# Weight splitting of the second layer done ahead of it: parts made during the first layer's MLP, kept in DRAM, loaded as parts

## The chip, the cores and the metric

The kernel runs on one core of one Trainium2 chip. The metric is the device time of one execution in microseconds (us). TensorE (PE) multiplies matrices; VectorE (DVE) and ScalarE (ACT) do elementwise work and empty the matmul results; GpSimd (POOL) computes a few reciprocal roots; SyncE (SP) issues almost all DMAs. Each engine takes its instructions in one fixed order and waits at the first one that isn't ready.

## The reference

Two layers of a decoder trunk over 1024 tokens of width 1024, all in float32. For each layer:

```
h = rms_norm(x, g_pre_mix);  z = h @ w_in            # one projection for three head groups
mix = concat(mLSTM(z), sliding_window_GQA(z), differential_attention(z)) @ w_out
x = x + rms_norm(mix, g_post_mix)
h2 = rms_norm(x, g_pre_mlp); u = square(relu(h2 @ w_up))
x = x + rms_norm(u @ w_down, g_post_mlp)
```

w_in has 2824 columns, w_up and w_down have 4096 hidden units.

## The kernel before

Every large matmul is computed from a high and a low part of both operands, so that the product keeps nearly float32 accuracy: `hi` is the value cast to the matmul's type (float32r), `lo` is the remainder, and the three products hi·hi, hi·lo and lo·hi are summed in PSUM. A weight tile is therefore a pair. It is made by `load_w` (line 103): for each half of 512 columns a DMA on SP brings the plain weights into a `raw` buffer (line 109, tensor `rw`), ACT casts them to `hi` (line 93) and DVE subtracts to get `lo` (line 94). There are two `raw` buffers of 512 columns, so one tile of 1024 columns can be waiting in plain form while its final buffers are still in use; the load then needs no final buffer, only the cast and the subtraction do. For w_up the cast also multiplies by a gain (lines 116 and 117).

Each layer runs in this order. First come the projections: `proj_tiles` (matmul line 286, tensors `wt`, results `pt`) for 13 tiles of w_in, in groups of one to four; `p_g2` (matmuls `pg`, weights `wg`, line 358) for the gates and values; `nat_group` (matmuls `pn`, weights `wv`) for two groups more. Differential attention (`diff1` to `diff4`) has the higher priority and is spread between the projections. Then sliding-window attention (`swa1`, `swa2`) and the mLSTM (`mlstm1` to `mlstm3`) run side by side, with the first half of the output projection (`out_group`, matmul line 849, weights `wo`, `woh`, `wol`); its second half follows with the post-norm (`post_mix`). Then the MLP runs in eight chunks of four hidden tiles: an up phase of 192 matmuls (line 1013, results `pu`, emptied on ACT at line 1016 as `r`) and a down phase of 192 (line 1058, results `pd`, added to `acm` on DVE at line 1069, or copied on ACT at line 1067 in the first chunk).

The final buffers of weights come from small pools: `whl` has two pairs, `wd` and `ws` four single tiles each. Most groups of projections use both `whl` pairs, so the next group's first tile can only be written when the running group has finished with a pair. The `mm` pool gives `pu`, `pt`, `pg` and `pn` two PSUM buffers; the down phase has four.

The order of each engine is set by a scheduler that walks the program with priorities (`ahead(n)` raises them) and fills free places of an engine with whatever is ready and has lower priority, however much later it stands in the source.

Of the kernel before, what the change touches and what calls it, by code (L numbers as in the profile page):

```python
# [10 lines left out]
F32 = mybir.dt.float32  # L11
F32R = mybir.dt.float32r
# [5 lines left out]
P = 128  # L18
# [16 lines left out]
def hybrid_kernel(ctx: ExitStack, tc: tile.TileContext, x_in, w_t, w_g, w_v, w_out, w_up, w_down,  # L35
                  pb, cv, gains, g_mlp, rope_t, masks, out):
    nc = tc.nc
# [9 lines left out]
    def pool(tag, bufs, space=None):  # L47
        kw = {} if space is None else {"space": space}
        pools[tag] = ctx.enter_context(tc.tile_pool(name="p_" + tag, bufs=bufs, **kw))
# [11 lines left out]
    pool("ys", 1)  # L61
    pool("mo", 1)
    pool("yy", 2)
    pool("mm", 2, PSUM)
    pool("ad", 2, PSUM)
    pool("as", 2, PSUM)
# [6 lines left out]
    def new(tag, shape, name, dt=F32):  # L73
        return pools[tag].tile(list(shape), dt, name=name, tag=tag)
# [13 lines left out]
    def ahead(n):  # L88

        return tc.high_priority(offset=n) if n else nullcontext()  # L90
# [5 lines left out]
    def load_split(hi, lo, src):  # L96
# [3 lines left out]
        nc.scalar.copy(hi, raw)  # L100
        nc.vector.tensor_sub(lo, raw, hi.bitcast(F32))

    def load_w(hi, lo, src, step, gain=None):


        for c in range(0, hi.shape[1], step):
            with ahead(1000):
                r = new("raw", (P, step), "rw")
                nc.sync.dma_start(r, src[:, c:c + step])
            with ahead(1000):  # L110
                if gain is None:
                    split(hi[:, c:c + step], lo[:, c:c + step], r)
                    continue
                for j in range(step // P):
                    cs, rj, g = slice(c + j * P, c + j * P + P), r[:, j * P:j * P + P], gain[:, c // P + j:c // P + j + 1]
                    nc.scalar.activation(hi[:, cs], rj, AF.Copy, scale=g)  # L116
                    nc.vector.scalar_tensor_tensor(out=lo[:, cs], in0=rj, scalar=g, in1=hi[:, cs].bitcast(F32),  # L117
                                                   op0=ALU.mult, op1=ALU.subtract)

    x_tiles = {}  # L120

# [81 lines left out]
    for j in range(4):  # L203
        if j == 1:
            load_x(1)
        r = new("wd", (P, 2, 392), "wg0")
# [11 lines left out]
    for l in range(DEPTH):  # L218
        lam_init = 0.8 - 0.6 * math.exp(-0.3 * l)
        last_layer = l == DEPTH - 1  # L220
# [36 lines left out]
        def proj_tiles(*groups):  # L257


            wts = []  # L260
            for idx, _, _, _, wtag in groups:
                for i in idx:
                    if wtag == "whl":
                        w = new("whl", (P, 2, 1024), "wt", F32R)
                        hi, lo = w[:, 0], w[:, 1]
                    else:
                        hi, lo = (new(wt_, (P, 1024), "wt", F32R) for wt_ in wtag)
                    load_w(hi, lo, w_t[l, i], 512)
                    wts.append((hi, lo))
            for half in range(2):  # L270
                wi = iter(wts)
                for idx, evac, tables, rtag, _ in groups:
                    if tables is not None:
                        with ahead(1000):
                            tab = new(rtag[1], (P, 2, 512), "tab")
                            nc.sync.dma_start(tab, rope_t[tables, :, :, half * 512:(half + 1) * 512])
                    qs = []
                    for i in idx:
                        hi, lo = next(wi)
                        q = PS("mm", "pt")  # L280
                        n = 0
                        for k in range(8):
                            kc = slice(k * P, (k + 1) * P)
                            for a, b in ((hi[:, kc], hT[half][:, :, kc]), (hi[:, kc], lT[half][:, :, kc]),
                                         (lo[:, kc], hT[half][:, :, kc])):
                                nc.tensor.matmul(q, lhsT=a, rhs=b, start=n == 0, stop=n == 23)  # L286
                                n += 1
                        qs.append(q)
                        if tables is None:
                            with ahead(1000):  # L290
                                evac(i, half, q)
                    if tables is not None:
                        with ahead(1000):
                            evac(half, qs, tab, rtag[0])
# [151 lines left out]
        dst = {}  # L446
# [247 lines left out]
        def nat_group(idx, evac):  # L694
            wv = []
            for j in range(2):
                w = new("whl", (P, 2, 1024), "wv", F32R)
                load_w(w[:, 0], w[:, 1], w_v[l, idx, :, 1024 * j:1024 * j + 1024], 512)
                wv.append(w.rearrange("p s (k c) -> p s k c", k=4))
            for t in range(NT):  # L700
                q = PS("mm", "pn")
                nat_mm(q, t, lambda k: (wv[k // 4][:, 0, k % 4], wv[k // 4][:, 1, k % 4]), 256)
                with ahead(1000):
                    evac(t, q[:, 0:256])
# [118 lines left out]
        def out_group(k0, slots, first, fin):  # L823
            wo = []
            nk = 4
            for k in range(nk):
                if slots[k] == "whl":
                    w = new("whl", (P, 2, DM), "wo", F32R)
                    hi, lo = w[:, 0], w[:, 1]
                else:  # L830
                    hi = new(slots[k], (P, DM), "woh", F32R)
                    lo = new(slots[k], (P, DM), "wol", F32R)
                kt = mix_kt[k0 + k]
                load_w(hi, lo, w_out[l, kt * P:(kt + 1) * P, :], 512)
                wo.append((hi, lo))
            for t in range(NT):
                ts = slice(t * P, (t + 1) * P)
# [6 lines left out]
                for n in range(2):  # L844
                    q = PS("mm", "po")
                    i = 0
# [89 lines left out]
        def p_g2():  # L936
            for k in range(8):
                if k < 4:
                    w = new("ws", (P, 2, 392), "wg", F32R)
                else:  # L940
                    if k % 2 == 0:
                        w2 = new("whl", (P, 2, 2, 392), "wg", F32R)
                    w = w2[:, k % 2]
                if l == 0:
                    split(w[:, 0], w[:, 1], wg0[k // 2][:, k % 2])
                else:
                    load_w(w[:, 0], w[:, 1], w_g[l, :, k, :], 392)
                wg.append(w)
            for t in range(NT):
                if l == 0 and t + 1 < NT:  # L950
                    first_norm(t + 1)
                g2(t)
            gating()
# [68 lines left out]
        utag = ("e", "e", "e", "e", "at", "at", "pt", "pt")  # L1022
        ptag = ("ad", "ad", "pvd", "pvs")
        ffs = [list(range(c * 4, c * 4 + 4)) for c in range(8)]
        for c in range(len(ffs)):
            final = c == len(ffs) - 1
            nf = len(ffs[c])
# [2 lines left out]
            for f in range(nf):  # L1030
                w = new("whl", (P, 2, 1024), "wu", F32R)
# [9 lines left out]
            for f in range(nf):  # L1041
                r0 = ffs[c][f] * P
                hi = new("wd", (P, DM), "wdh", F32R)
                lo = new("ws", (P, DM), "wdl", F32R)
# [29 lines left out]
            def post_mlp(t):  # L1074
# [19 lines left out]
                if not last_layer:  # L1094
                    pre_norm_transpose(a, gt[1], a, n_hT[t // 4], n_lT[t // 4], t % 4)

            head = groups[:4]
            qs4 = [PS(ptag[j], "pd") for j in range(4)]
            cnt = [0] * 4
# [103 lines left out]
```

## Time and profile before

| | us |
|---|---|
| median of 3 runs (lowest, highest) | 2480.98 (2479.06, 2483.18) |
| the profiled execution's own time | 2487.86 |
| its span, first to last instruction | 2486.1 |
| first layer's mixer | about 0 to 558 |
| first layer's MLP | about 558 to 1228 |
| second layer's mixer | about 1228 to 1791 |
| second layer's MLP | about 1791 to 2457 |

The span is 1.8 us shorter than that execution's time, and the execution is 6.9 us above the median of the runs. A matmul's busy time is counted from its start to a modelled end, and matmuls overlap, so PE shows busy in almost all of the span; the distance from one matmul to the next is the better measure. In the MLP 192 matmuls take 43.52 us, 0.2267 us each.

### The profile page before, as it was taken

Reading aid. Unit: us, or ns where it says so; the run is one execution under the profiler, and the core shown is the slowest. Engines: PE = TensorE matmul, PEld = TensorE weight load, DVE = VectorE, ACT = ScalarE, POOL = GpSimd, SP = SyncE. Lnnn points to the kernel's source line nnn. Section 1 sums busy time; section 2 is a strip of 40 time slices with the busy share of each in tenths; the row PEclk is TensorE's granted clock in tenths of the full one; section 3 lists DMA queues with packets and bytes.
Section 4 is the critical chain, followed back from the end, with each engine's and each line's share of the span. In section 5 each row is a group of like instructions: output and inputs, shape, how many; then the busy total and the mean of one; then the engine's idle time right before and its main releaser. Section 6 shows DMA issues by size and latency. Waiting matters only on the chain.

```text
span 2486.1 us, 32491 instructions
## 1 busy us (share of the span) xinstructions
PE 2380.3 (96%) x11556; PEld 1977.1 (80%) x11556; DVE 1456.5 (59%) x3604; ACT 1074.4 (43%) x2657; POOL 91.3 (4%) x174
## 2 busy tenths in 40 slices
PE   8999979789999999999999999888899999999998
PEld 7889867668888888888778889766688888888887
DVE  5798978674334433543686988777734334434436
ACT  4356867464312321331434757765644123212312
POOL 0000000010000000000000001000100000000000
PEclk9999999899999999999999999989999999999999
DMA  4554253432101201210552453433322012101204
GB/s 166 176 181 133 72 155 98 104 121 68 51 26 60 68 29 40 68 51 26 169 179 86 137 169 109 135 101 96 119 68 68 26 43 68 51 26 60 68 26 161
DMA packets 146866, 227.42 MB, mean 91 GB/s; under 512 B 23376, under 2 KB 61456, under 8 KB 146704
## 3 DMA queue, kind: packets, MB, share of 16 engines
q1 hardware_dynamic: 144544, 221.70, 28.3%
q10 hardware_dynamic: 2160, 3.65, 0.4%
q8 instruction: 91, 1.49, 0.2%
q14 instruction: 71, 0.58, 0.1%
HBM read 179.09 MB, written 46.20 MB: 91 GB/s over the span
## 4 chain that ended last, share of the span: by engine, by line
PE 78%; DVE 8%; DMA 5%; ACT 4%; issue 2%; POOL 2%; SPq 0%; POOLq 0%; DVEq 0%; ACTq 0%
PE pu L1013 26%; PE pd L1058 26%; PE pt L286 9%; PE po L849 3%; PE pn L358 3%; PE pg L358 2%; POOL rs L153 2%; DMA mb<-m_rows 2%; PE pv L530 2%; PE sp L495 1%; PE trd L522 1%; DMA mxl<-mix_d 1%; PE ss L612 1%; ACT junk L159 1%; PE pvs L646 1%
## 5 line engine op out<-in xcount | busy, mean ns | idle before, releaser
L1013 PE MATMUL pu<-h2T,wu 128*128 128x512 f32 x3072 | 704.7, 391 | 0.8 <-ACT h2T L93 0.8
L1013 PEld LDWEIGHTS pu<-h2T,wu 128*128 128x128 f32 x3072 | 577.8, 188 | 122.4 <-DVE h2T L94 1.3
L1058 PE MATMUL pd<-wdh,u 128*128 128x512 f32 x2048 | 635.2, 390 | 1.6 <-DVE acm L1069 1.6
L1058 PEld LDWEIGHTS pd<-wdh,u 128*128 128x128 f32 x2048 | 384.7, 188 | 81.6 <-DVE acm L1069 2.0
L1058 PE MATMUL pd<-wdl,u 128*128 128x512 f32 x1024 | 399.0, 390 | 0.0
L1069 DVE TENSOR_TENSOR acm<-acm,pd 128x512 f32<-128x512 f32 x224 | 153.1, 686 | 309.2 <-PE pd L1058 309.2
L1016 ACT ACTIVATE r<-pu 128x512 f32<-128x512 f32 x128 | 75.2, 588 | 537.0 <-PE pu L1013 536.2
L286 PE MATMUL pt<-hT,wt 128*128 128x512 f32 x832 | 279.5, 401 | 2.0 <-DVE lamp L228 1.5
L116 ACT ACTIVATE wu<-rw,gk 128x128 fp32r<-128x128 f32 x512 | 160.3, 390 | 185.9 <-PE pu L1013 133.8
L117 DVE SCALAR_TENSOR_TENSOR wu<-rw,gk,wu 128x128 fp32r<-128x128 f32 x512 | 154.0, 350 | 140.1 <-ACT wu L116 140.1
L1058 PEld LDWEIGHTS pd<-wdl,u 128*128 128x128 f32 x1024 | 192.5, 188 | 39.9
L1019 DVE TENSOR_TENSOR r<-r 128x512 f32<-128x512 f32 x128 | 88.3, 690 | 221.5 <-ACT u L1018 221.5
L286 PEld LDWEIGHTS pt<-hT,wt 128*128 128x128 f32 x832 | 155.5, 190 | 31.0 <-issue 1.9
L286 PE MATMUL pt<-lT,wt 128*128 128x512 f32 x416 | 166.0, 399 | 0.0
L153 POOL TENSOR_TENSOR rs<-ms,mhalf 128x1 f32<-128x1 f32 (+2 forms) x112 | 79.4, 713 | 2284.3 <-DVE ms L151 2215.9
L94 DVE TENSOR_TENSOR wdl<-rw,wdh 128x512 fp32r<-128x512 f32 x128 | 88.5, 692 | 106.4 <-ACT wdh L93 106.3
L849 PE MATMUL po<-woh,mxl 128*128 128x512 f32 x384 | 134.8, 410 | 8.2 <-DVE acc L857 6.6
L93 ACT CAST wdh<-rw 128x512 fp32r<-128x512 f32 x128 | 79.3, 619 | 131.6 <-DMA rw<-in_w_down_dram 131.5
L501 ACT ACTIVATE e<-e,nb 128x256 f32<-128x256 f32 (+7 forms) x128 | 99.4, 777 | 37.8 <-DVE nb L498 37.3
L358 PE MATMUL pn<-wv,hT 128*128 128x256 f32 x512 | 106.5, 289 | 0.2 <-ACT mv L708 0.2
L849 PEld LDWEIGHTS po<-woh,mxl 128*128 128x128 f32 x384 | 73.3, 194 | 22.9 <-DVE acc L857 7.9
L1020 DVE TENSOR_TENSOR u<-r,u 128x512 fp32r<-128x512 f32 x128 | 88.5, 691 | 4.0
(225 smaller groups left out, 3329.2 us busy)
## 6 DMA issues: line engine op xcount, KB each, us to landing
rw<-in_w_up_dram SPq DMA_DIRECT2D x128, 256.0 KB, 2.9
rw<-in_w_down_dram SPq DMA_DIRECT2D x128, 256.0 KB, 2.8
rw<-in_w_t_dram SPq DMA_DIRECT2D x52, 256.0 KB, 3.0
tab<-in_rope_dram SPq DMA_DIRECT2D x20, 512.0 KB, 4.4
xt<-in_x_dram SPq DMA_DIRECT2D x16, 512.0 KB, 4.2
d_rope<-rot SPq DMA_DIRECT2D x32, 256.0 KB, 3.2
s_ropeq<-rot SPq DMA_DIRECT2D x32, 256.0 KB, 2.7
qq<-s_ropeq SPq DMA_DIRECT2D x16, 512.0 KB, 5.0
```

Of the source, the lines that this page charges most:

```text
L94: nc.vector.tensor_sub(lo, src, hi.bitcast(F32))
L116: nc.scalar.activation(hi[:, cs], rj, AF.Copy, scale=g)
L117: nc.vector.scalar_tensor_tensor(out=lo[:, cs], in0=rj, scalar=g, in1=hi[:, cs].bitcast(F32), op0=ALU.mult, op1=ALU.subtract)
L153: nc.gpsimd.tensor_tensor(out=rs, in0=ms, in1=mhalf[:, 0:n], op=ALU.pow)
L286: nc.tensor.matmul(q, lhsT=a, rhs=b, start=n == 0, stop=n == 23)
L358: nc.tensor.matmul(q[:, 0:n], lhsT=a, rhs=b, start=i == 0, stop=i == 23)
L501: nc.scalar.activation(e[:, 0:L], e[:, 0:L], AF.Exp, bias=nb[:, nch - 1:nch], scale=-1.0, accum_out=den[:, m:m + 1])
L849: nc.tensor.matmul(q, lhsT=mx[:, a, k], rhs=wo[k][b][:, n * 512:(n + 1) * 512], start=i == 0, stop=i == 3 * nk - 1)
L1013: nc.tensor.matmul(q, lhsT=w[:, a, kc], rhs=h2[b + half][:, :, kc], start=n == 0, stop=n == 23)
L1020: nc.vector.tensor_sub(us[1][:, hs], r, us[0][:, hs].bitcast(F32))
L1058: nc.tensor.matmul(q, lhsT=U[f][a][:, t * P:(t + 1) * P], rhs=D[f][b][:, n * 512:(n + 1) * 512], start=i == 0, stop=i == 3 * nf - 1)
L1069: nc.vector.tensor_add(a, a, q)
```

## The change

`pre_pieces` lists 58 pieces of the second layer's weights: 8 of 392 columns for `wg`, 26 of 512 for `wt`, 8 for `wv`, 16 for w_out. `pre_split` treats one: it loads the plain piece into a buffer `r`, casts it on ACT into a buffer `h`, subtracts on DVE in place, and stores both parts to DRAM tensors (`pre_t`, `pre_g`, `pre_v`, `pre_o`). `r` and `h` share a new pool `pre` of two buffers, so a piece's load waits until the piece before has stored its low part. In the source nine pieces stand in each of the first layer's MLP chunks, between the up and the down phase, until all 58 are used up. The second layer calls `load_pair` in place of `load_w`: two DMAs of 128x1024 (or 128x392) values, one for each part, straight into the final buffers.

```diff
+    pool("pre", 2)
+    def load_pair(hi, lo, src):
+        with ahead(1000):
+            for s, d in enumerate((hi, lo)):
+                nc.sync.dma_start(d.bitcast(F32), src[:, s])
+    pre_t = pr.tile([13, P, 2, 1024], F32, name="pre_t")
...
+    def pre_split(src, dst):
+        n = src.shape[1]
+        r = new("pre", (P, 512), "pr")[:, 0:n]
+        h = new("pre", (P, 512), "ph", F32R)[:, 0:n]
+        nc.sync.dma_start(r, src)
+        nc.scalar.copy(h, r)
+        nc.vector.tensor_sub(r.bitcast(F32R), r, h.bitcast(F32))
+        nc.sync.dma_start(dst[0], h.bitcast(F32))
+        nc.sync.dma_start(dst[1], r)
...
-                    load_w(hi, lo, w_t[l, i], 512)
+                    if l == 0:
+                        load_w(hi, lo, w_t[l, i], 512)
+                    else:
+                        load_pair(hi, lo, pre_t[i])
...
-                    load_w(w[:, 0], w[:, 1], w_g[l, :, k, :], 392)
+                    load_pair(w[:, 0], w[:, 1], pre_g[k])
...
+        pieces = [] if last_layer else list(pre_pieces())
         for c in range(len(ffs)):
...
+            for j in range(9 if c < 7 else 0):
+                if pieces:
+                    pre_split(*pieces.pop(0))
             head = groups[:4]
```

`wv` and w_out are changed in the same way as `wt`. Line numbers shift: what is line 286 before is line 328 after, 358 is 400, 849 is 897, 1013 is 1061, 1016 is 1064, 1018 is 1066, 1058 is 1107, 1067 is 1116; the piece's load, cast, subtraction and stores are lines 153 to 157, `load_pair` is line 108.

The scheduler doesn't leave the pieces where the source has them. Of the 58 casts, 27 stand in ACT's order before the first evacuation of an up phase of the first layer, that is in the first layer's mixer, the first of them among the first norms; the other 31 stand in the first two chunks of the MLP and the beginning of the third. The places are these.

On ACT, at the end of the first chunk's up phase and in its down phase, before:

```order
L1016 ACTIVATE r<-pu 128x512
L116 ACTIVATE wu<-rw,gk 128x128 x4
L1018 ACTIVATE u<-r 128x512
L116 ACTIVATE wu<-rw,gk 128x128 x8
L1067 COPY acm_6100<-pd 128x512 x8
L1067 COPY acm_6101<-pd 128x512 x8
L1016 ACTIVATE r<-pu 128x512
```

and after (`ph<-pr` is the cast of a piece):

```order
L1064 ACTIVATE r<-pu 128x512
L154 CAST ph<-pr 128x512
L123 ACTIVATE wu<-rw,gk 128x128 x4
L1066 ACTIVATE u<-r 128x512
L123 ACTIVATE wu<-rw,gk 128x128 x8
L154 CAST ph<-pr 128x512
L1116 COPY acm_6109<-pd 128x512 x5
L154 CAST ph<-pr 128x512
L1116 COPY acm_6109<-pd 128x512 x2
L154 CAST ph<-pr 128x512
```

One cast of a piece now stands between evacuations of an up phase, and one after every second copy of a down phase; in the next chunk's down phase the subtractions stand in the same way between DVE's `acm` additions.

On PE, in the second layer, where `p_g2` ends and the first group of `p_m` begins, before:

```order
L358 MATMUL pg<-wg,lT_6105 128x392
L495 MATMUL sp<-ks,qs 128x384
L495 MATMUL sp<-ks,qs 128x512
L286 MATMUL pt<-hT_6102,wt 128x512
L286 MATMUL pt<-lT_6104,wt 128x512
L286 MATMUL pt<-hT_6102,wt 128x512 x2
L286 MATMUL pt<-lT_6104,wt 128x512
L286 MATMUL pt<-hT_6102,wt 128x512 x2
L286 MATMUL pt<-lT_6104,wt 128x512
L495 MATMUL sp<-ks,qs 128x512
L286 MATMUL pt<-hT_6102,wt 128x512
L401 MATMUL pgt<-gtmp,mk 128x32
```

and after:

```order
L400 MATMUL pg<-wg,lT_6114 128x392
L537 MATMUL sp<-ks,qs 128x256 x4
L537 MATMUL sp<-ks,qs 128x384 x2
L328 MATMUL pt<-hT_6111,wt 128x512
L443 MATMUL pgt<-gtmp,mk 128x32
L328 MATMUL pt<-lT_6113,wt 128x512
L447 MATMUL put<-mk,u_g 32x128
L328 MATMUL pt<-hT_6111,wt 128x512
L537 MATMUL sp<-ks,qs 128x512
L328 MATMUL pt<-lT_6113,wt 128x512
L453 MATMUL pcm<-mk,cmt 128x32
L456 MATMUL prep<-gtmp,mk 128x64
```

Before, `pt` matmuls follow each other here; now only two of each tile stand ahead of the small matmuls of the gates (`pgt` to `prep`), and six of attention (`sp`) come first.

On SP, in the second layer, where the weights of the second half of the output projection are loaded, before:

```order
L109 DMA rw<-in_w_out_dram 128x512 x2
L991 DMA xt_16447<-x_new 128x1024
L751 DMA mb_14727<-m_g 128x256
L109 DMA rw<-in_w_out_dram 128x512 x2
L991 DMA xt_16512<-x_new 128x1024
L109 DMA rw<-in_w_out_dram 128x512 x2
```

and after:

```order
L108 DMA woh<-pre_o 128x1024
L108 DMA wol<-pre_o 128x1024
L108 DMA woh<-pre_o 128x1024
L108 DMA wol<-pre_o 128x1024
L1039 DMA xt_16696<-x_new 128x1024
L1039 DMA xt_16761<-x_new 128x1024
L108 DMA woh<-pre_o 128x1024
L108 DMA wol<-pre_o 128x1024
L108 DMA woh<-pre_o 128x1024
L108 DMA wol<-pre_o 128x1024
```

Six plain loads of 256 KB that alternate with others have become eight loads of 512 KB in one run, and each waits for PE to be done with the buffer that it writes.

More of the change, by code (lines that the diff above doesn't have):

```diff
@@ L118, in load_w, with pre_pieces @@
                                                    op0=ALU.mult, op1=ALU.subtract)
+    pr = ctx.enter_context(tc.tile_pool(name="pr", bufs=1, space=bass.MemoryType.DRAM))
+    pre_t = pr.tile([13, P, 2, 1024], F32, name="pre_t")
+    pre_g = pr.tile([8, P, 2, 392], F32, name="pre_g")
+    pre_v = pr.tile([2, 2, P, 2, 1024], F32, name="pre_v")
+    pre_o = pr.tile([8, P, 2, 1024], F32, name="pre_o")
+    def pre_pieces():
+        for k in range(8):
+            yield w_g[1, :, k, :], [pre_g[k, :, s] for s in range(2)]
+        for i in range(13):
+            for c in range(0, 1024, 512):
+                yield w_t[1, i, :, c:c + 512], [pre_t[i, :, s, c:c + 512] for s in range(2)]
+        for g in range(2):
+            for j in range(2):
+                for c in range(0, 1024, 512):
+                    yield w_v[1, g, :, 1024 * j + c:1024 * j + c + 512], [pre_v[g, j, :, s, c:c + 512] for s in range(2)]
+        for k in range(8):
+            for c in range(0, 1024, 512):
+                yield w_out[1, k * P:(k + 1) * P, c:c + 512], [pre_o[k, :, s, c:c + 512] for s in range(2)]
+    def pre_split(src, dst):
[7 more added lines that the diff above has]
+        nc.sync.dma_start(dst[1], r)
     x_tiles = {}
@@ L697, in nat_group @@
                 w = new("whl", (P, 2, 1024), "wv", F32R)
-                load_w(w[:, 0], w[:, 1], w_v[l, idx, :, 1024 * j:1024 * j + 1024], 512)
+                if l == 0:
+                    load_w(w[:, 0], w[:, 1], w_v[l, idx, :, 1024 * j:1024 * j + 1024], 512)
+                else:
+                    load_pair(w[:, 0], w[:, 1], pre_v[idx, j])
                 wv.append(w.rearrange("p s (k c) -> p s k c", k=4))
@@ L833, in out_group @@
                 kt = mix_kt[k0 + k]
-                load_w(hi, lo, w_out[l, kt * P:(kt + 1) * P, :], 512)
+                if l == 0:
+                    load_w(hi, lo, w_out[l, kt * P:(kt + 1) * P, :], 512)
+                else:
+                    load_pair(hi, lo, pre_o[kt])
                 wo.append((hi, lo))
```

## The prediction

> **What bounds the kernel now.** I read the chain of waits first, for the pace of PE; then the table of busy times by stage; then the DMA issues and the single groups for durations. In the chain the first layer's MLP reads:
>
> ```profile
> 558.62 34.74 PE pu L1013 x144
> 593.36 43.52 PE pd L1058 x192
> ```
>
> 192 matmuls take 43.52 us, 0.2267 us each, and nothing else stands in the chain there. The stages (columns: window, its length, busy time and instructions of PE, PE's weight loads, DVE, ACT, POOL, then PE's granted clock, the share of the DMA engines, GB/s):
>
> ```profile
> 57.00:310.00 253.00, 249.75 (x1448) 211.26 (x1447) 211.58 (x586) 149.44 (x389) 14.37 (x30) 1.00 0.44 140
> 310.00:558.00 248.00, 209.19 (x1056) 165.90 (x1054) 185.28 (x558) 160.34 (x424) 21.88 (x39) 0.94 0.41 120
> 558.00:1180.00 622.00, 621.62 (x2736) 513.93 (x2734) 253.82 (x504) 180.67 (x422) 0.00 (x0) 1.00 0.15 49
> 1180.00:1283.00 103.00, 95.80 (x440) 77.26 (x440) 76.54 (x132) 44.97 (x86) 9.62 (x16) 0.98 0.48 164
> 1283.00:1560.00 277.00, 274.09 (x1591) 237.69 (x1589) 222.75 (x636) 160.47 (x425) 15.54 (x39) 1.00 0.42 133
> 1560.00:1791.00 231.00, 197.81 (x1019) 159.59 (x1017) 174.41 (x532) 150.58 (x400) 19.89 (x30) 0.93 0.40 117
> ```
>
> Three kinds of stage. In the MLP PE has no gap, and DVE and ACT are busy for 41% and 29%. In the projections (57 to 310 and 1283 to 1560) PE lacks 3 us in 253 and 2.9 in 277 although DVE is busy for 80% or more: PE is the limit, and relief on DVE can give back only those 2.9 us. In the attention and mLSTM stage of the second layer (1560 to 1791) PE lacks 33 us, and between the layers (1180 to 1283) 7; only there can less work on DVE or ACT shorten the second layer.
>
> **What the change removes.** In the second layer, 58 casts and 58 subtractions, at these prices:
>
> ```profile
> L93 ACT CAST wt<-rw x26: 603/620/635, 1208.8 to 1451.8; 128x512 fp32r<-128x512 f32 x26
> L94 DVE TENSOR_TENSOR wt<-rw,wt x26: 654/684/693, 1209.5 to 1453.0; 128x512 fp32r<-128x512 f32 x26
> L93 ACT CAST woh<-rw x12: 604/620/622, 1576.4 to 1709.6; 128x512 fp32r<-128x512 f32 x12
> ```
>
> 58 x 0.62 = 36 us of ACT and 58 x 0.68 = 39 us of DVE. By far the most lies beside a PE that doesn't stop. In the stages with gaps lie the 16 casts of w_out (11 us of DVE) and some six of the first `wt` tiles. They are spread over chains that also run through PE, DMA and POOL; from the 40 us of PE gaps I take a gain of 7, between 0 (they lie beside other waits) and 15 (all 11 us of DVE and the first `wt` tiles' share come off the end).
>
> **What it adds in the first layer's mixer.** 27 pieces, 27 x 0.68 = 18 us on DVE and 17 on ACT, in places that the order left free. DVE has 41 us free in 57 to 310 and 63 in 310 to 558, so most is covered; where a piece meets a chain it costs one cast and one subtraction, 1.3 us. SP waits in its order for each piece's two stores, and the `rw` loads of `wt` tiles 1 to 3 now stand behind the fifth to seventh piece; by the piece's period below they come 2 to 4 us later than before, about as much as the tiles are early. I take 4 us, between 0 (all in free places) and 12 (nine of the 27 meet a chain).
>
> **What it adds in the first layer's MLP.** ACT and DVE have room for 31 x 1.3 us. The question is the period of one piece, since `pre` has two buffers: load, cast, subtraction, store of the low part, and only then the next load. The parts:
>
> ```profile
> rw<-in_w_down_dram SPq DMA_DIRECT2D x128, 256.0 KB, 2.8
> s_ropeq<-rot SPq DMA_DIRECT2D x32, 256.0 KB, 2.7
> m_qk<-yc SPq DMA_DIRECT2D x16, 256.0 KB, 2.1
> ...
> 2457.38 1.41 DVE L1087 SCALAR_TENSOR_TENSOR ag<-ag,rs,xt 128x512 f32<-128x512 f32 x2
> 2458.16 1.00 SPq L1088 DMA_DIRECT2D out_dram<-ag  x2
> ```
>
> Load 2.8, cast 0.62, subtraction 0.68, store between 2.1 and 2.7, taken as 2.4 since two stores of a piece go together; four hand-overs between engines of 0.08 (the first of the two DVE instructions ends at 2458.08, its store is issued at 2458.16). Together 6.8 us; 6.2 with the quickest store and no hand-over; 7.5 with a store as slow as the load plus a wait of 0.4 on SP. Now the order: in the MLP one cast of a piece stands between two evacuations of an up phase, which are 24 matmuls or 5.44 us apart, and one after every second evacuation of the first down phase, also 5.44 us. ACT can't empty `pu` before the piece in front of it has been loaded, so pieces that come every 6.8 us hold back a PE that could go on every 5.44. What saves it is slack: two PSUM buffers in the up phase and four in the down phase, and a few places without a piece. Counted in the order, the cast of the 28th piece stands behind PE's last work before the up phase, and the 58th holds back a `pu` matmul in the third chunk; between these two points lie 840 matmuls, 840 x 0.2267 = 190 us, for 30 periods. 30 x 6.8 + 1.5 for the evacuation that follows = 205.5: PE comes 15 us late. At a period of 6.2 or less it is nothing, at 7.5 it is 36. I take 14.
>
> **What it adds in the second layer.** Before, plain halves waited in `raw`, and once a final buffer was free a tile cost a cast and a subtraction, 1.3 us for each half. Now the free buffer is followed by 1 MB of DMA. The nearest rows:
>
> ```profile
> qq<-s_ropeq SPq DMA_DIRECT2D x16, 512.0 KB, 5.0
> tab<-in_rope_dram SPq DMA_DIRECT2D x20, 512.0 KB, 4.4
> lT<-x_mid SPq DMA_DIRECT2D x8, 512.0 KB, 5.6
> ```
>
> `qq` are two loads of 512 KB issued together, as a pair is; 1 MB in 5.0 to 5.6 us. From 256 KB in 2.8 to 512 KB in 4.4 is 1.6 us for one load alone, while pairs overlap; for 2 MB at once I take 9 us, for 1.5 MB 7. Against this stands the PE work between the last matmul that read a buffer and the first that needs its new contents, counted in the new order. For most `wt` tiles this is 7.0 to 13 us: covered. It isn't at these places, with the cover and what is missing: the first `p_m` group (2 MB into both `whl` pairs, third load needed after 3.5 us of PE work: 4), the last `wg` tile (2.4: 1), the second `wv` tile (2.6: 3), the next `wv` pair (3.1: 3), the first w_out pair in `whl` (4.2, second tile at 9 us: 3), and the last two w_out tiles in `wd` (4.5, behind two loads of `xt` and two pairs on the same queue: 4). Together 18 us. Every matmul behind the waiting one waits too, so in the projections this is lost in full. The lower bound is 6, if pairs land as one load does and half of the waits fall on gaps that exist; the upper 30, with 12 us for 2 MB as four loads in a row would need.
>
> [...]
>
> **Sum.** 4 + 14 + 18 - 7 = 29 us on the profiled execution: a span of 2515. That execution took 2487.86 us, 1.8 more than its span and 6.9 more than the median of the runs, so against the median 2480.98 + 29 = 2510.
>
> **Rivals.**
> - *The pieces don't hold PE back.* If loads and stores in the otherwise quiet MLP (15% DMA share) come at 6.2 us or less, the 14 falls away: 2496. For it speaks that ACT and DVE are mostly idle there; against it that each part of the period has a row, and only the quickest store gets there.
> - *Relief wins: faster.* DVE's 74% and ACT's 64% in 1560 to 1791 pace the attention and mLSTM chains, where PE lacks 33 us. Freed of 16 pairs of instructions, they give back 11 us, the start of the second layer gives 4 and its projections lose no more than those 2.9 us hold; with nothing lost in the first layer that is 2466. It decides as soon as the waits for pairs total less than 11 us and the piece's period is below 6.3. Against it: in 1283 to 1560 a PE without gaps can only lose, and there stand 11 of the 18 us.
> - *Everything is hidden.* PE's work is the same, and the scheduler has put both the pieces and the pairs where it sees room: 2481.
>
> **How the numbers follow.** Forecast 50%, first rival 20%, second 18%, third 8%; 4% for a loss beyond the bounds. What a measurement of this kernel can tell from no change is about 0.2%, 5 us. The forecast's own range is 2496 to 2535 (its terms' ends rarely meet). Eight times in ten: from 2470, inside the faster case, to 2545, where a period of 7.5 us adds 22 to the forecast and waits another 13. Slower: 50 + 20 + 4 = 74%; no difference 8%; faster 18%.
>
> **What would show it.** For the MLP: between 558 and about 760 PE's share falls below 95%, `r<-pu` on ACT waits behind `ph<-pr`, whose group shows waits for the DMA of `pr`, and casts of pieces follow each other at 6.5 to 7.2 us; after the last piece, chunks take 87.04 us again. For the second layer: PE waits for DMA of `wt`, `wv`, `wo` and `woh` appear, the largest after the last `pg` matmul, and the stage from there to the end of the projections lasts longer by about 10 us. For the relief: DVE's busy time in the second layer's mixer is 39 us lower, and the stage after it up to 7 us shorter. The forecast is wrong if the first MLP keeps its 43.52 us a phase from the start, or if PE's gaps in the second layer's projections stay near 3 us.

## The result, and the profile after

The change is slower: 2525.73 us median (2525.68 to 2526.65) against 2482.08 (2479.06 to 2483.25) for the kernel before on the same chip, a ratio of 1.0179 with a 95% interval of 1.0161 to 1.0196. The profiled execution of the change took 2525.69 us, as its median; that of before took 2487.86, so the two traces differ by less (37.6 us of span) than the medians (43.7). The experiments show where the missing 6 us are: seven kernels (e2 to e7 and e10) whose PE, ACT and DVE do the same in the first mixer, in the same order, reach the first down phase 2.8 to 6.7 us earlier than the trace of before, 4.9 on average. So the traced execution of before was slow in its first mixer.

The two traces are best compared at the starts of down phases, which are read from the records of PE:

| start of | before | change | later by |
|---|---|---|---|
| first MLP, first down phase | 593.2 | 607.5 | 14.3 |
| second | 680.2 | 701.3 | 21.1 |
| fourth | 854.3 | 879.5 | 25.1 |
| last | 1202.5 | 1227.6 | 25.1 |
| second layer, first down phase | 1825.5 | 1863.1 | 37.6 |
| last | 2434.8 | 2472.4 | 37.6 |

So 14.3 us (about 19 against a usual execution of before) were lost by the first down phase, 10.8 in the next three chunks, 12.5 between the two MLPs, and nothing in the second MLP.

**In the first mixer.** The chain of waits of the change (start, length, what):

```profile
79.32 5.15 DMA pr<-in_w_g_dram
84.65 0.53 ACT ph L154
85.20 0.57 DVE pr L155
85.77 0.61 DVE rot L357
```

DVE stood at a piece's subtraction until the piece had been loaded and cast, with the rotary work of the projections (`rot`) behind it. Over the mixer, in the waits (engine, what, what it waited for: total, times, longest):

```profile
ACT ph L154 <- DMA pr<-in_w_g_dram: 18.0, 7, 7.6
DVE pr L155 <- ACT ph L154: 8.6, 6, 2.8
SPq L156 <- ACT ph L154: 33.2, 13, 4.7
```

All three queues stand still for pieces: ACT for the load, DVE for the cast, and SP for the cast, with the loads of the next weights behind the stores. The 18.0 us of ACT belong to the first eight pieces. For the 19 that follow, ACT waited 4.5 us.

These waits are not the loss itself. By the count of PE's matmuls the change is 5.5 us behind before at 120 us, and still about 6 behind at 340; the other 8 us of the 14.3 come between 340 and 560, in the attention and mLSTM stage. There one load of a piece stands in the chain (at 417.43, 7.74 us), but loads that belong to no piece are slow as well: those of `mxl`, between 310 and 600, land after 5.3 us (median) in place of 2.5. Whether the place of the pieces in the order or their traffic makes this second part is open: e3 and e4 below take both out of the mixer at once.

**In the first MLP.** The chain again:

```profile
594.09 4.28 DMA pr<-in_w_t_dram
599.47 3.35 DMA pre_t<-ph
602.84 3.15 DMA pr<-in_w_t_dram
608.47 3.60 DMA rw<-in_w_up_dram
614.38 2.95 DMA pre_t<-ph
617.40 3.58 DMA pr<-in_w_t_dram
622.66 35.30 PE pd L1107 x144
...
719.94 2.52 DMA pre_o<-ph
722.48 2.67 DMA pr<-in_w_out_dram
725.95 2.27 DMA pre_o<-ph
```

Loads and stores of pieces follow one another as one serial chain, mixed with loads of the MLP's own weights (`rw`). After 710 (and from 629 to 669), where few other loads run, a piece takes about 5.9 us (719.94 to 725.95, 6.0, is one); where the MLP's own loads come between, the casts are 7.2 to 7.8 us apart (the first two are 9.2 apart). From the first cast in the MLP (574.3) to the last (771.9) lie 30 periods, 6.59 us in the mean. PE stopped at two places, by the timeline (start, length, instruction, idle time before it and what ended it):

```profile
618.13 0.39 PE L1107 MATMUL pd<-wdh,u 128*128 128x512 f32 x1
622.66 0.79 PE L1107 MATMUL pd<-wdh,u 128*128 128x512 f32 x1 [4.14 <-ACT acm L1116]
...
714.49 0.50 PE L1107 MATMUL pd<-wdh,u 128*128 128x512 f32 x1 [2.13 <-DVE acm L1118]
```

The first stop is 4.14 us, yet the second down phase comes 6.8 us later. The rest is in the clock. By windows (columns as in the prediction; the eighth is the granted clock):

```profile
622.66:627.52 4.86, 4.86 (x11) 3.79 (x12) 0.19 (x1) 1.40 (x3) 0.00 (x0) 0.50 0.60 188
627.52:658.00 30.48, 30.48 (x135) 25.27 (x134) 3.59 (x6) 10.18 (x17) 0.00 (x0) 1.00 0.38 134
```

After the stop PE ran for 4.86 us at half its clock, 11 matmuls at 0.43 us each in place of 0.2267, some 2.4 us more. Behind the stop of 2.13 us only one matmul was slow. Over the whole trace PE's gaps add up to 110.6 us against 86.6, 24.0 more; the other 13.6 of the 37.6 us are matmuls that stood further apart while PE ran. By the clock records of the two traces, about 11 of these are matmuls at half clock; the rest is not attributed.

**In the second layer.** Four of the uncovered pairs stand in the chain:

```profile
1334.94 32.74 PE pg L400 x183
1367.71 5.79 DMA wt<-pre_t
...
1568.03 6.62 DMA wv<-pre_v
1621.51 6.00 DMA wo<-pre_o
1757.71 7.74 DMA wol<-pre_o
```

A step of the chain is not PE's loss: PE did other matmuls meanwhile, and its idle time put down to pairs is 6.4 us in the whole of the second layer's mixer (1.8 for `wt`, 0.9 for `wv`, 3.7 for w_out). The one behind the last gate matmul (`pg`) costs most, since PE's clock is 0.50 for the 6 us after it:

```profile
1360.00:1368.00 8.00, 7.92 (x46) 7.71 (x44) 1.77 (x9) 1.01 (x3) 0.00 (x0) 1.00 0.03 8
1368.00:1374.00 6.00, 3.35 (x10) 1.90 (x11) 4.39 (x23) 3.35 (x15) 0.00 (x0) 0.82 0.90 294
1374.00:1380.00 6.00, 5.72 (x17) 4.00 (x17) 3.39 (x20) 1.36 (x5) 0.10 (x1) 0.50 0.26 97
```

The DMA engines had been almost idle (0.03) while `pg` held the buffers, and were 90% busy as soon as they were free. At equal work, that is at the same amount of matmul work done, PE is 24.5 us late before this place and 32.6 after it. For the stretch from the last down phase of the first MLP to the first of the second, before and after:

```profile
1202.50:1825.50 623.00, 579.60 (x3091) 483.96 (x3090) 480.98 (x1312) 360.74 (x920) 45.05 (x85) 0.97 0.42 130
1227.60:1863.10 635.50, 584.31 (x3091) 485.71 (x3090) 454.39 (x1256) 331.58 (x863) 45.03 (x85) 0.97 0.46 149
```

PE's gaps grow from 43.4 to 51.2 us, which is 7.8 of the 12.5; the other 4.7 are matmuls further apart.

### The profile page after: what moved, and what is told of

Its sections match the earlier page's. It is cut to its first block, busy times and chain, and to the rows that moved or that the text cites. A ratio compares the mean times of both kernels' runs of the same rounds, so it can differ in the third digit from the quotient of the medians.

```text
span 2523.7 us, 32848 instructions
## 1 busy us (share of the span) xinstructions
PE 2393.7 (95%) x11556; PEld 1987.6 (79%) x11556; DVE 1460.3 (58%) x3604; ACT 1077.8 (43%) x2657; POOL 91.4 (4%) x174
## 4 chain that ended last, share of the span: by engine, by line
PE 71%; DMA 12%; DVE 8%; ACT 4%; issue 2%; POOL 2%; SPq 1%; POOLq 0%; ACTq 0%; DVEq 0%
PE pu L1061 24%; PE pd L1107 23%; PE pt L328 8%; PE po L897 3%; PE pn L400 2%; DMA mb<-m_rows 2%; PE pg L400 2%; POOL rs L192 2%; PE pv L572 2%; DMA mxl<-mix_d 1%; PE trd L564 1%; PE sp L537 1%; DMA rw<-in_w_up_dram 1%; DMA rw<-in_w_down_dram 1%; DMA pr<-in_w_out_dram 1%
## 5 line engine op out<-in xcount | busy, mean ns | idle before, releaser
L328 PEld LDWEIGHTS pt<-lT,wt 128*128 128x128 f32 x416 | 79.8, 192 | 13.5
```

## The experiments

All times are set against runs of the kernel before on the same chip. The last three columns say how much later than in the trace of before the kernel was at the first down phase of the first MLP, and how much it lost from there to that MLP's last down phase, and from there to the second layer's first. (The first of them has to be read against -4.9, the mean of kernels with an unchanged first mixer; in e8, e9, e11 and e12 more raw buffers give the mixer another order.)

| | median us | ratio, 95% interval | first mixer | first MLP | second layer's mixer |
|---|---|---|---|---|---|
| the change | 2525.7 | 1.0179 [1.0161, 1.0196] | 14.3 | 10.8 | 12.5 |
| e1 pieces alone | 2512.6 | 1.0124 [1.0102, 1.0146] | 16.6 | 10.7 | 0.8 |
| e2 pairs alone | 2536.3 | 1.0216 [1.0190, 1.0242] | -2.8 | 40.8 | 11.4 |
| e3 pieces in down phases | 2506.0 | 1.0100 [1.0076, 1.0123] | -5.0 | 9.5 | 13.6 |
| e4 serial in the MLP | 2520.4 | 1.0148 [1.0123, 1.0173] | -6.1 | 24.7 | 7.5 |
| e5 pieces on POOL | 2524.1 | 1.0181 [1.0162, 1.0200] | -4.2 | 26.2 | 9.3 |
| e6 covered pairs only | 2499.8 | 1.0084 [1.0067, 1.0101] | -6.7 | 12.3 | 4.3 |
| e7 first group split | 2509.6 | 1.0115 [1.0097, 1.0134] | -3.4 | 30.3 | -5.7 |
| e8 four raw buffers | 2484.2 | 1.0019 [1.0010, 1.0028] | -2.2 | 3.8 | -7.0 |
| e9 before, four raw buffers | 2489.8 | 1.0041 [1.0028, 1.0054] | -2.2 | 2.2 | -1.6 |
| e10 as e8, two raw buffers | 2490.6 | 1.0052 [1.0038, 1.0066] | -6.1 | 14.3 | -6.1 |
| e11 three raw buffers | 2475.3 | 0.9979 [0.9969, 0.9988] | -7.3 | 0.0 | -5.2 |
| e12 before, three raw buffers | 2484.5 | 1.0018 [1.0008, 1.0028] | -4.6 | 0.0 | 2.3 |

### e1: the pieces without the pair loads

```diff
-                    if l == 0:
-                        load_w(hi, lo, w_t[l, i], 512)
-                    else:
-                        load_pair(hi, lo, pre_t[i])
+                    load_w(hi, lo, w_t[l, i], 512)
```

and in the same way for `wv`, `wg` and w_out.

> The pieces are made and stored in the first layer as in the change, but the second layer splits its plain weights as before; the stored parts are not read. Theory (from the two traces): the change's 37.6 us on the profiled executions are 14.3 in the first mixer, 10.8 in the first MLP and 12.5 behind it; here the first two stay and the last is gone, so PE reaches the third chunk's up phase of the first MLP about 25 us later than before and the time is 2481 + 25 = 2506, with a ratio of 1.010. Rival A (the second layer's pair loads are the main loss, and what the first layer loses is mostly slack that comes back at the layer boundary): below 2490. Rival B (the traffic of the pieces in the first layer is the whole loss): above 2518.

Measured 2512.6. The first layer loses what it does in the change (16.6 and 10.7), the second nothing (0.8), and PE's order there is that of before. It lies 6 us above the expectation, which was worked out against the slow trace of before: 16.6 + 4.9 + 10.7 + 0.8 is 33, and the medians differ by 32.3. Both rivals fall: the first layer's loss does not come back, and it isn't the whole.

### e2: the pair loads without the pieces

```diff
-            for j in range(9 if c < 7 else 0):
-                if pieces:
-                    pre_split(*pieces.pop(0))
+            if pieces:
+                h = new("pre", (P, 512), "ph", F32R)
+                nc.scalar.copy(h, W[3][:, 0, 0:512].bitcast(F32))
+            for j in range(9):
+                if pieces:
+                    for d in pieces.pop(0)[1]:
+                        nc.gpsimd.dma_start(d, h[:, 0:d.shape[1]].bitcast(F32))
```

> The second layer loads pairs from DRAM as in the change, but the first layer makes no pieces: one rounded 128x512 tile per chunk of the MLP is stored into every part by POOL's DMA queue, so no casts, subtractions or loads of pieces are left and the second layer computes with other weights. Theory: the uncovered pair loads cost about 21 us and the relief of DVE and ACT gives 9 back, net +12, 2493, ratio 1.005. Rival A (relief wins as soon as the first layer is left alone): 2470 or less. Rival B (all of the change's 44 us of medians come from the second layer): 2520 or more.

Measured 2536.3. That lies in the range of rival B (2520 or more), but not for its reason: the second layer did not make it, the first MLP lost 40.8 us to my stores. Its chain, at the end of the second chunk's up phase:

```profile
667.55 8.05 DMA rw<-in_w_down_dram
...
683.56 2.56 DMA rw<-in_w_down_dram
```

A burst of stores stretched single weight loads from 2.6 to 8 us, and the MLP, with a DMA share of 15% in before, had no slack for it. The part of the experiment that answers the question is the second layer: 11.4, near the change's 12.5, although nothing was lost in the first mixer. That loss belongs to the pair loads, together with the order of PE that the scheduler makes with them (the same in the change and in e2 to e5; e1 has that of before).

### e3 and e4: the pieces out of the mixer

e3 takes the pieces' tiles from the pool of six evacuation buffers:

```diff
-        r = new("pre", (P, 512), "pr")[:, 0:n]
-        h = new("pre", (P, 512), "ph", F32R)[:, 0:n]
+        r = new("ev", (P, 512), "pr")[:, 0:n]
+        h = new("ev", (P, 512), "ph", F32R)[:, 0:n]
```

> All that the change does, but the two tiles of a piece come from the pool of six evacuation buffers instead of a pool of two: three pieces can be under way at once, and none can be moved into the first mixer, since the pool is in use there in the program's order; nine pieces stand in each down phase. Theory (a piece costs PE only because the next load waits for the store before it, and because it is hoisted into the mixer): the first layer loses nothing, the second 12, together 2493, ratio 1.005. Rival (58 casts, 58 subtractions and 44 MB of traffic cost wherever they stand): the first layer still loses 15 to 25, 2508 to 2518.

e4 keeps the pool of two and makes it wait for the first chunk:

```diff
+            if c == 0 and not last_layer:
+                for _ in range(2):
+                    z = new("pre", (P, 512), "pz", F32R)
+                    nc.scalar.copy(z, U[3][0][:, 0:512].bitcast(F32))
             for j in range(9 if c < 7 else 0):
```

> As the change, with two buffers for the pieces, but the two buffers are first written from a result of the first MLP's first chunk, so that no piece can start in the mixer: all 58 run one behind the other in the MLP. Theory (serial period): each piece takes about 5.9 us (load 2.6, cast and subtraction 0.9, store 2.3) against places 5.44 us of PE work apart; 58 x 0.46 = 27 us, less the slack of the PSUM buffers and of places without a piece, so the first MLP loses 12 to 25 us, each of its gaps lengthened by a lowered clock, and the mixer nothing; with 12 for the second layer 2505 to 2518. Rival (the MLP lost its 11 us only because the mixer ended in disorder, with its weights late): the first layer loses nothing, 2493.

In both the mixer's loss is gone (-5.0 and -6.1): it was made by the hoisted pieces. e3 took 2506.0 us, between its theory and its rival; e4 took 2520.4, a little above its range of 2505 to 2518. In the MLP the serial pieces of e4 cost 24.7, the upper end of what was expected of them; its rival, that the MLP only inherited the mixer's disorder, falls. e3's three pieces at a time cost 9.5, not the 0 of the theory and not the 15 or more of the rival. What is left there, from PE's waits between 545 and 1215:

```profile
PE pd L1106 <- DVE acm L1117: 7.2, 6, 1.8
```

one stop in each of the chunks two to seven, each time for the first evacuation of a down phase on DVE.

### e5: the pieces on an idle engine

```diff
-        nc.sync.dma_start(r, src)
-        nc.scalar.copy(h, r)
-        nc.vector.tensor_sub(r.bitcast(F32R), r, h.bitcast(F32))
-        nc.sync.dma_start(dst[0], h.bitcast(F32))
-        nc.sync.dma_start(dst[1], r)
+        nc.gpsimd.dma_start(r, src)
+        nc.gpsimd.tensor_copy(out=h, in_=r)
+        nc.gpsimd.tensor_sub(r.bitcast(F32R), r, h.bitcast(F32))
+        nc.gpsimd.dma_start(dst[0], h.bitcast(F32))
+        nc.gpsimd.dma_start(dst[1], r)
```

with the wait of e4, its copies on POOL too.

> All that the change does, but a piece's load, cast, subtraction and stores are all issued and computed by POOL, which has no work in the MLP, one piece behind the other, and none before the first chunk of the first MLP (as in e4_serial_in_mlp). Theory (a piece costs only through the engine that stands still for its load, with the mixer's rope work or the MLP's evacuations queued behind it): the first layer loses nothing, the second about 12 as in e1 to e4 (12.5, 11.4, 13.6 and 7.5 between the end of the first MLP and the second): 2493, ratio 1.005. Rival A (the pieces' 44 MB of traffic slow the weight loads of the MLP): the first MLP loses 10 to 20 as in e4, 2503 to 2513. Rival B (the second layer's loss was caused by the disorder that the first left): 2481.

Measured 2524.1: the theory that a piece costs only through the engine that stands still for it is wrong. No piece stands in ACT's, DVE's or SP's order here, and the first MLP still loses 26.2, more also than rival A's 10 to 20. The chain of e5 ahead of the second down phase's stop:

```profile
685.62 3.79 DMA rw<-in_w_up_dram
...
689.86 2.67 DVE wu L124 x4
692.53 0.61 DVE acm L1118
693.18 35.10 PE pd L1107 x144
```

and in before the same place on DVE, by the timeline:

```profile
687.27 1.23 DVE L117 SCALAR_TENSOR_TENSOR wu<-rw,gk,wu 128x128 fp32r<-128x128 f32 x4 [0.39 <-ACT wu L116]
689.28 1.37 DVE L1069 TENSOR_TENSOR acm<-acm,pd 128x512 f32<-128x512 f32 x2 [0.78 <-PE pd L1058]
```

This is a constraint that the prediction did not see. The next chunk's weights (`wu`) are split on DVE ahead of the first evacuation (`acm`) of the running one, through two raw buffers. In before the last of these splits is done 0.78 us before PE has the first result ready (0.5 to 0.8 in chunks two to seven). PE wants the freed PSUM buffer 1.8 us after that result (the 48 head matmuls end 10.9 us into the phase, the first evacuation starts 9.04 into it), and the evacuation takes 0.69, so the whole slack is 0.78 + 1.8 - 0.69, about 1.9 us. By estimate from these numbers, a few weight loads that take half a microsecond longer each would use that up, and then every chunk would stop; that the chain of loads is the limit is tested below, by more raw buffers. In e5 DVE itself was slower as well; the groups between 600 and 1060, in e5 and in before (total, mean ns):

```profile
L124 DVE SCALAR_TENSOR_TENSOR wu<-rw,gk,wu 128x128 fp32r<-128x128 f32 x164 | 56.7, 399 | 41.5 <-ACT wu L123 40.9 <-PE pd L1107 0.6
L1068 DVE TENSOR_TENSOR u<-r,u 128x512 fp32r<-128x512 f32 x40 | 32.7, 816 | 1.3
```

```profile
L117 DVE SCALAR_TENSOR_TENSOR wu<-rw,gk,wu 128x128 fp32r<-128x128 f32 x168 | 50.5, 350 | 42.1 <-ACT wu L116 42.1
L1020 DVE TENSOR_TENSOR u<-r,u 128x512 fp32r<-128x512 f32 x40 | 27.7, 692 | 1.3
```

The same instructions take 14 to 18% longer while POOL computes pieces. How much of the 26.2 is DVE and how much the loads is open.

### e6 and e7: which pairs cost

e7 is e5 with one more condition, e6 splits `wv` and four w_out tiles as well:

```diff
-                    if l == 0:
+                    if l == 0 or i in (9, 10):
                         load_w(hi, lo, w_t[l, i], 512)
```

> As e5, but only the tiles whose pair load has, in the new order, at least 6 us of PE work between the buffer's release and the first use come as pairs (all of w_g, eleven of the thirteen w_t tiles, four of the eight w_out tiles: 38 pieces); the first two w_t tiles behind the gates, all of w_v and four w_out tiles are split in the second layer as before. Theory (the second layer loses at uncovered loads alone): no loss, and of the relief of 30 casts and 30 subtractions at most a few us show, since PE lacks almost nothing in the projections: 2474 to 2483, ratio 0.998 to 1.001. Rival (pairs cost through their doubled bytes wherever they are): still 6 to 12 slower, 2487 to 2493.

> As e5, but the first two w_t tiles behind the gates (1.4 and 1.8 us of cover in the new order, 2 MB of pairs) are split in the second layer as before. Theory (the wait behind the last gate matmul, 5.8 us in the chain of the change, and the lower clock after it): 6 to 8 us faster than e5, so a ratio of 1.002 if e5 has 1.005. Rival (this wait only takes the place of another that ends later): the same as e5.

e7 is 14.6 us below e5, although its first MLP lost 4 more: the second layer's mixer goes from +9.3 to -5.7. At the place itself, in the chain of e5 and then of e7:

```profile
1332.38 32.74 PE pg L400 x183
1365.15 5.59 DMA wt<-pre_t
```

```profile
1337.03 32.76 PE pg L400 x183
1369.79 0.25 PE sp L537 x2
1370.14 3.32 DMA rw<-in_w_t_dram
```

At equal work PE loses 7.4 us there in e5 and 0.7 in e7, as expected. The other 8 us appear in the attention stage, where PE's order differs between the two kernels; e3 and e10 differ in the same way there. Which wait makes them is open.

That e7 is shorter there than before is not shown to be the relief of DVE and ACT. The same stretch in e10, where PE's order is that of e7:

```profile
1210.70:1827.60 616.90, 573.33 (x3091) 478.44 (x3090) 451.80 (x1258) 333.99 (x867) 45.30 (x85) 0.98 0.47 151
```

DVE is busy for 29 us less than in before, yet PE's gaps are 43.6 us against 43.4 (43.5 in e7, 43.6 in e8, 44.8 in e11). What is shorter is PE's own time, 573.3 against 579.6: its matmuls stand closer together, at a higher granted clock (0.98 against 0.97).

e6 is off both its expectations (2499.8): its MLP loses 12.3 with 38 pieces, and its second layer +4.3 with fewer pairs than e7, where e7 has -5.7. So the rule by which I chose its tiles (at least 6 us of cover) isn't the one that decides outside the projections, and what e7 gains comes with the pairs of `wv` and w_out that e6 left out.

### e8 to e12: a version with slack for the pieces

e8 joins e3 and e7's condition, leaves the first chunk without pieces, emits them behind the head evacuations, and spends what the pool `pre` took:

```diff
-    pool("raw", 2)
+    pool("raw", 4)
-    pool("pre", 2)
...
             for j, (t, n) in enumerate(head):
                 down_evac(qs4[j], t, n)
+            for j in range(9 if 0 < c < 7 else 0):
+                if pieces:
+                    pre_split(*pieces.pop(0))
```

e10 is e8 with two raw buffers, e11 with three; e9 and e12 are the kernel before with four and three.

> As e3 (pieces through the six evacuation buffers, in the down phases), with the first two w_t tiles behind the gates split as in e7, the pieces only in chunks 1 to 6, and the 4 KB that the pool of the pieces no longer takes given to two more buffers for raw weights (four instead of two). Theory: in the MLP of before the last split of a weight ends 0.5 to 0.8 us ahead of the first evacuation of a down phase, so the chain of loads through two raw buffers has no slack for the pieces' traffic; with four buffers it has, and the first MLP loses nothing (e3: about 9); the second layer is between -6 and +4 as in e7 and e6: 2475 to 2485, ratio 0.998 to 1.002. Rival (the stalls in the down phases come from the subtractions of pieces that stand ahead of evacuations on DVE, not from the weight loads): the MLP still loses 6 to 9, 2485 to 2494.

> The kernel before with four buffers for raw weights instead of two and nothing else: what e8 gets from them alone. Theory: the MLPs of before have no gap to give back, the projections 6 us and the attention stages about 30 each, few of them for weights: 2474 to 2482, ratio 0.997 to 1.000. Rival (raw loads pace the mixers too): 2465 or less.

> As e8, with two raw buffers as before: the step between e3 and e8. Theory: the first MLP loses 6 to 9 again (stalls of 1.4 to 1.8 us in each of chunks 1 to 6), the wait behind the gates is gone: 6 to 8 below e3, 2497 to 2500, ratio 1.007; and 10 above e8. Rival (the raw buffers don't matter): the same as e8.

> As e8, with three buffers for raw weights instead of four. Theory: the chain of weight loads of the MLP has slack with three as with four, so the pieces cost no more than the 2 us of e8's first MLP; the second layer's relief without the group behind the gates gives 6 as in e7, e8 and e10 (-5.7, -7.0 and -6.1 from the end of the first MLP to the start of the second); what the fourth buffer costs in the mixer and the MLPs (e9 is 10 above before) shrinks by half: 2478 to 2482, ratio 0.999 to 1.001. Rival (three are too few for the pieces' traffic): 2488 as e10.

> The kernel before with three buffers for raw weights: the kernel that e11 has to be set against. Theory: half of e9's loss, 2483 to 2487, ratio 1.002, so that the parts from DRAM, made and loaded in this way, are worth 3 to 6 us. Rival (the buffers alone make the difference): the same as e11.

The raw buffers decide what the pieces cost: with the same 54 pieces in the same chunks the first MLP loses 14.3 with two buffers (more than the 6 to 9 that I expected), 3.8 with four (2.2 of them also without pieces, in e9) and nothing with three. The chain of e11 through its chunks with pieces:

```profile
629.59 43.52 PE pu L1060 x192
673.11 43.52 PE pd L1106 x192
```

and its DVE at the place shown for before and e5:

```profile
673.59 2.40 DVE L123 SCALAR_TENSOR_TENSOR wu<-rw,gk,wu 128x128 fp32r<-128x128 f32 x8 [3.16 <-ACT wu L122]
...
681.03 0.57 DVE L154 TENSOR_TENSOR pr<-pr,ph 128x392 fp32r<-128x392 f32 x1 [2.36 <-ACT ph L153]
681.99 1.37 DVE L1117 TENSOR_TENSOR acm<-acm,pd 128x512 f32<-128x512 f32 x2 [0.39 <-PE pd L1106]
```

The last split of `wu` now ends 2.9 us into the down phase (673.11) in place of 8.3, two pieces fit in before the first evacuation, and DVE still waits for PE. The scheduler made this order by itself once there was a third buffer.

e11 is faster than before: 0.9979, interval 0.9969 to 0.9988, 5.7 us of medians, at the limit of what a measurement here tells apart. The third buffer alone (e12) makes the kernel 3.5 us slower, so against its own control the parts from DRAM are worth 9 us by the medians; e8 against e9 gives 5.7. On the traces 7.5 us of e11's gain over e12 lie in the second layer's mixer and 2.7 in the first, where both kernels do the same in the same order. e8 (2484.2) and e12 (2484.5) came out in their ranges; e10 came out 6 us below its range and e11 3 us below, and the parts are worth more than the 3 to 6 us of e12's expectation. The expectation that more buffers alone cost nothing (e9) was wrong, and why they cost 3.5 and 10 us is open.

## Why the prediction was right or wrong

**Sign and size.** Slower was right, for the reasons given in kind; 2510 was 16 us too low. By its terms, against the usual execution of before:

| term | predicted (bounds) | measured |
|---|---|---|
| pieces in the first mixer | 4 (0 to 12) | 14.3 on the traces, about 19 against a usual mixer; above its bounds |
| pieces in the first MLP | 14 (0 to 36) | 10.8 |
| second layer: waits for pairs less relief | 18 - 7 = 11 | 12.5 |

**The step that failed is the first mixer's.** It priced a piece that meets a chain at one cast and one subtraction, 1.3 us. What a piece costs there is also the wait for its load, because its instructions stand in a fixed order: ACT stood 18.0 us in seven waits for the first pieces alone, each up to 7.6, DVE and SP behind it, and PE was 5.5 us late at 120 us. e3 and e4 take the pieces out of the mixer and the loss goes with them; how the 8 us of the attention stage are shared between order and traffic stays open. The free places on DVE (41 and 63 us) were the wrong thing to count: the load wasn't ready when the place came.

**The first MLP's term held, and it hid a second cause.** Its 30 periods took 197.6 us, 6.59 each, where 6.8 were predicted; put into the prediction's count (30 x 6.59 + 1.5 - 190) they make PE 9 us late, and 10.8 were measured, a part of it by the lower clock (0.50 for 4.86 us, some 2.4 us). The period is made of another mixture than said, though: about 5.9 us where the pieces' chain is alone, 7.2 to 7.8 where SP has the MLP's own weight loads between a piece's store and the next piece's load. That the mean comes so near 6.8 is luck: the parts were priced too high, and the MLP's own loads on the queue were left out. And the period is not all that counts. In before, the chain that splits these weights has only about 1.9 us of slack at the evacuation behind it: e5, without a piece in any order but POOL's, loses 26 us, and e11, with a third raw buffer, nothing. "DVE and ACT are busy for 41% and 29%" and a DMA share of 15% told of capacity, where the limit was a latency.

**The second layer** was right in its largest place and close in its sum, but its two terms are not shown. The place behind the last `pg` matmul is the dearest in the projections, as said: 8 us at equal work, where 4 stood. From there to the end of the projections PE loses about 13 us at equal work (10 predicted). But PE's idle time put down to pairs is 6.4 us where 18 was said (what follows from these stops, such as the clock of 0.50 in 1374 to 1380, is not in it), and of the 12.5 only 7.8 are gaps; so 11 against 12.5 is in part luck. Nor do the runs show the relief as the prediction has it, as shorter gaps of PE. With the one worst group split again, the second layer's mixer is 5.2 to 7.0 us shorter than before in e7, e8, e10 and e11, with gaps of PE that are no smaller in sum, by matmuls closer together. Only against e12 has e11 shorter gaps too (44.8 us against 49.1, one trace each). The subtractions that are gone took 39 us in all in the trace of before, as said, but DVE's busy time falls by 26.5 us only (447.20 in 1205 to 1829 against 473.70 in 1180 to 1791): the busy time counts instructions that overlap once.

**The price of a pair.** The prediction took 5.0 to 5.6 us for a pair, from loads that go two together in before, and 9 us for 2 MB. The issues of the change:

```profile
wt<-pre_t SPq DMA_DIRECT2D x26, 512.0 KB, 4.9
wol<-pre_o SPq DMA_DIRECT2D x6, 512.0 KB, 6.2
```

These go two or more at a time; how much of their time is the sharing of the engines is not shown. The measurement stands above the row of 4.4 for a single load. The two pairs behind the last `pg` matmul, 2 MB in four loads, were issued from 1366.65 on, and the DMA engines were busy until about 1375.5 (share 0.56 in 1374 to 1375, 0.12 in the next us, then 0.00): about 9 us, as said. The 12 us for 2 MB in the upper bound were the author's estimate; no run shows them.

**What was to be seen.** 43.52 us a phase came back after the pieces, from the fourth chunk on (right). PE's share in 558 to 760 below 95% (just missed: 192.37 of 202, 95.2%, with the late end of the mixer in it; 97% in 572 to 836). Casts 6.5 to 7.2 us apart (right in the mean, 6.59; singly from 5.5 to 9.2).

**The rivals.** "The pieces don't hold PE back" falls: 6.2 us or less was reached only where the chain ran alone. "Relief wins" named its condition, waits for pairs under 11 us and a period below 6.3; neither held (the second layer lost 12.5 us with its relief already in it, and the period was 6.59). e11 comes nearest to it: with the worst group split again and the first layer free the kernel is faster, 2475 where the rival gave 2466, but not by the shorter gaps of PE that the rival named.

**Not in the sum at all** was the clock: 13.6 of the 37.6 us are matmuls further apart, not gaps, and about 11 of these lie at half clock. The trace of before had it in sight, with a granted clock of 0.94 and 0.93 in the two stages where PE has most of its gaps, and 1.00 where it has next to none.

## What to carry to other kernels

Work that waits for a DMA was not free here, although its engine had idle time: ACT stood 18.0 us for the first eight pieces, and what came behind them in its order waited too. So a scheduler that moves such work into a free place must know when its data lands. Before adding traffic to a stage that "has room", look for the chain with the least slack in it (here about 1.9 us at an evacuation, through two buffers) and give that chain a buffer first, counting what the buffer costs by itself (3.5 us here). Replacing a short computation at the point of use by a longer load that can only start when the final buffer is free can turn prefetched work into exposed latency; e7 shows for one group that it pays to keep the computation where the buffer is released right before it is needed (PE loses 0.7 us there, 7.4 in e5). And look at the granted clock before crediting a gain to an engine that was relieved: in e10 PE's gaps stayed the same (43.6 us against 43.4), at a clock of 0.98 against 0.97.

## What the hardware showed that was not expected

- A stop of PE cost more than its length, and not in proportion to it. In the change, after 4.14 us without a matmul the granted clock was 0.50 for 4.86 us (matmuls 0.43 us apart in place of 0.2267); after 2.13 us only one matmul was slow. In before, at the end of the first MLP, PE stood for 2.03 us (until 1226.95), and soon after its clock was halved all the same:

```profile
1228.00:1231.20 3.20, 3.20 (x11) 2.61 (x10) 2.31 (x5) 2.87 (x6) 0.55 (x1) 0.50 0.72 200
```

  By the clock records the half clock of before lasted about 3.4 us here. A stop of 2.03 us was followed by it and one of 2.13 us was not, so how long a stop must be to bring it is not shown. Six short stops, of at most 1.8 us each, cost e3's MLP 9.5 us with 7.2 of them in the waits; behind the one that ended at 690.80 the next 132 matmuls took 30.21 us, 0.229 us each. One long one cost the change 6.8 with 4.1.
- Some of DVE's instructions took longer while POOL worked. With POOL casting and subtracting pieces (e5), DVE's 128x512 instruction `u` took 816 ns on average in place of 692, between 600 and 1060; in e11, where ACT and DVE treat the pieces and POOL is busy for 0.00 us in 586 to 1195, it took 691. The additions `acm` kept their time (684 in e5, 687 in before). What makes the others slower is not shown. POOL's own subtraction of 128x512 took 1357 ns, twice the 684 of DVE's for `wt` in before.
- In e2 a burst of stores on one queue went with longer loads on another: with some 18 stores of up to 256 KB issued by POOL for one chunk, two weight loads of 256 KB on SP, one after the other, took 8.05 us (from 667.55) and 5.17 us (from 677.00); the one before them took 2.96 us and the one behind them 2.56 us.
